# The down products of two ConvFFN channel mixers, by seven products of quarter blocks instead of a plain sum

## The chip, the cores and the metric

The kernel runs on one core of a Trainium2 chip. The metric is the device time of one execution in microseconds (us); lower is better. The engines are named as in the profile: PE (matrix products), DVE (vector), ACT (activations), POOL (GpSimd), and SP, whose queue issues the DMA transfers here.

## The reference

Two layers run over 1024 prompt frames and 64 sample frames (T = 1088 columns in the kernel, features on the partitions). Each layer is a token mixer (S5 in layer 0, forgetting attention in layer 1) followed by the channel mixer, with an RMSNorm in front of each and one at the end. The channel mixer is what the change touches:

```python
D_MODEL, D_FF = 1024, 2816
def conv_ffn(x, hist, w_up, w_gate, conv_w, conv_b, w_down):
    l = x.shape[1]
    a = x @ w_up
    a_pad = jnp.concatenate([hist.astype(a.dtype), a], axis=1)
    conv = a_pad[:, 0:l] * conv_w[0]
    for j in range(1, CONV_WIDTH):
        conv = conv + a_pad[:, j:j + l] * conv_w[j]
    h = jax.nn.gelu(conv + conv_b) * (x @ w_gate)
    return h @ w_down, a_pad[:, -(CONV_WIDTH - 1):]
```

All is float32. The kernel gets near float32 from the PE by splitting each operand into a high and a low part (`hi`, `lo`) and adding three matmuls: high by high, high by low, low by high.

## The kernel before

The 1088 columns are four chunks of 272 (`NCH`); columns 0 and 2 are half a = 0 and columns 1 and 3 half a = 1 (`HALVES`). The 2816 inner features are 22 tiles of 128 rows; two of them are a pair `fp`, so there are 11 pairs.

**Up and gate.** For each pair and for each of the two weights, `left_factors` loads 1024 x 256 weights into `raw` and makes the left factors of seven products of quarter blocks (the sums s1, a21, a11, a12 on POOL, each high part on ACT, each low part on POOL; the buffers `whi` and `wlo` hold three tiles each). `seven` runs the seven products for both halves a, so 14 products of 12 matmuls (4 slices of the inner dimension by 3), which share the PSUM banks A, B, G and H of each half. ACT copies bank A after products 0, 2 and 4 into a `tm` tile (5 buffers), and `put` adds a bank and a copy on DVE. Then `convolve` (DVE L424) and the gate product (L454) follow; the gated row h is split into a high part (ACT) and a low part (DVE L456), and both go to DRAM (`hD`), 0.557 MB each.

**Down.** `load` brings the rows back into the tiles `E` and `R` (28 in all), which hold the normalised input of up and gate until the last gate product has read them. The 22 tiles are taken in chunks of 3 (the last of 4, `FCH`); for each chunk, each of 8 output tiles d and each column chunk n, `down_tile` sums 9 (or 12) matmuls in one bank and DVE adds it to the residual x (L482). In the last chunk the columns go outermost, and as soon as one column chunk is complete, `norm.add` sums its squares and `after(n)` yields the steps that work on it: in layer 0 `to_operands`, which makes the normalised operands of the next product (`qkv`); in layer 1 `final`, which scales, transposes and writes the output.

The order of instructions on each engine is set by a scheduler, not by the lines of the source: it moves a later product ahead of an earlier one where it sees fit. SP issues the transfers in one queue, in order.

Of the kernel before, what the change touches and what calls it, by code (L numbers as in the profile page):

```python
# [16 lines left out]
P = 128  # L17
# [11 lines left out]
FCH = ((0, 3), (3, 3), (6, 3), (9, 3), (12, 3), (15, 3), (18, 4))  # L29
# [114 lines left out]
class Norm:  # L144
# [55 lines left out]
    def to_operands(self, i, g):  # L200

        k = self.k
        nc = k.nc
        o, n = NCH[i]
        r = self.inverse(i)
        yield
        yield
        pb = self.spread(i, r)
        for d in range(KT):
            t = k.tmp.tile([P, CW], F32, name="tm")[:, :n]  # L210
            nc.vector.scalar_tensor_tensor(t, k.x[d][:, o:o + n], k.gains[:, g, d:d + 1], pb, op0=OP.mult, op1=OP.mult)
            h = k.xh[d][:, o:o + n]
            nc.scalar.activation(h, t, AF.Copy)
            (nc.gpsimd if d % 4 else nc.vector).tensor_tensor(k.xl[d][:, o:o + n], t, h.bitcast(F32), op=OP.subtract)
# [76 lines left out]
def left_factors(k, w, c0):  # L291
# [3 lines left out]
    raw = k.wraw.tile([P, KT, 2 * P], F32, name="raw")  # L295
    nc.sync.dma_start(raw, w[:, c0:c0 + 2 * P].rearrange("(k p) c -> p k c", p=P))
    a11, a12, a21, a22 = (raw[:, 4 * i:4 * i + 4, P * f:P * f + P] for f in range(2) for i in range(2))

    def split(t, pools, shape, name):
        h, l = (q.tile(shape, F32R, name=name[i]) for i, q in enumerate(pools))  # L300
        nc.scalar.activation(h, t, AF.Copy)  # L301
        add(l, t, h.bitcast(F32), op=OP.subtract)  # L302
        return [[(h[:, 4 * i + kt], l[:, 4 * i + kt]) for kt in range(4)] for i in range(shape[1] // 4)]

    pair = (k.whi, k.wlo), [P, KT, P], ("hi", "lo")
    p1, p2 = split(raw[:, :, 0:P], *pair)
    s1 = k.idle[:, 0:4 * P].rearrange("p (a b) -> p a b", b=P)
# [4 lines left out]
    p6, p3 = split(raw[:, :, 0:P], *pair)  # L312
    p7, p4 = split(raw[:, :, P:2 * P], *pair)
    p5, = split(s1, (k.ws, k.ws), [P, 4, P], ("s1h", "s1l"))
# [3 lines left out]
def seven(k, left, halves, put, steps=None):  # L318
# [11 lines left out]
    def product(j, a, bank):  # L330
        more = j in (2, 4, 6)
        for kt in range(4):
            h, l = left[j][kt]
            rh, rl = (k.form(j, p, a)[:, kt] for p in range(2))
            for i, (x, y) in enumerate(((h, rh), (h, rl), (l, rh))):
                nc.tensor.matmul(bank[:, :CW], x, y, start=not more and kt == 0 and i == 0, stop=kt == 3 and i == 2, skip_group_check=True)  # L336
# [33 lines left out]
def ffn(k, layer, norm, after, prepare=lambda: None):  # L370
# [4 lines left out]
    hD = [k.dram.tile([2, P, T], F32, name=f"hD{layer}_{f}") for f in range(FT)]  # L375
    NX = 4
    cw = k.cw[layer]
    with ExitStack() as ctx:
# [6 lines left out]
        E, R = [(k.E[2 * i], k.E[2 * i + 1]) for i in range(6)], [(k.R[2 * i], k.R[2 * i + 1]) for i in range(8)]  # L385
        slots = E + R + E[:2] + R[:2] + E[2:]

        def load(fs):
            for f in fs:
                for t, src in zip(slots[f], (hD[f][0], hD[f][1])):  # L390
                    nc.sync.dma_start(t.bitcast(F32), src)

        def down_unit(ci, u, to=None):
            f0, nf = FCH[ci]
            src = w_down[f0 * P:(f0 + nf) * P, :].rearrange("(f p) c -> p f c", p=P)
            return unit(k, src[:, :, 2 * u * P:2 * (u + 1) * P], nf, 2 * P, to=to)

        def channels(fp, steps):
# [33 lines left out]
            if steps is not None:  # L432
                seven(k, left_factors(k, w_up, c0), ((0,),), put_up, steps)
                seven(k, left_factors(k, w_gate, c0), ((0,), (1,)), put_gate)
# [1141 lines left out]
```

## Time before, and how its profile reads

| | |
|---|---|
| median of 3 runs | 2755.19 us (2753.61 to 2761.34) |
| profiled execution: time, span | 2759.6 us, 2757.8 us |
| PE busy | 2632.0 us, 95% of the span |
| DVE, POOL, ACT busy | 57%, 53%, 39% |
| up and gate of layers 0 and 1 | about 470 to 977 and 1980 to 2460 us |
| down of layers 0 and 1 | about 977 to 1250 and 2460 to 2745 us |

The last two lines are rounded from the first and last instructions of `seven` and of `down_tile`. A share of busy time is a mean over stages with different limits, so it has to be asked for by stage. A wait counts only where PE stands still for it.

### The profile page before, as it was taken

The page shows a single profiled execution, that of the slowest core. Times are in us where ns is not written, and L with a number is a line of the kernel's source. Part 1 is how long each engine was busy: PE and PEld are TensorE (multiplying, and loading weights), DVE is VectorE, ACT ScalarE, POOL GpSimd, SP SyncE. Part 2 cuts the span into 40 slices and gives each one's busy share as a digit, 9 for nine tenths or more (in the row PEclk, how much of TensorE's full clock was granted, in tenths as well). Part 3 has the DMA queues.
Part 4 walks back from the last instruction along what each step waited for, and adds up shares of the span by engine and source line. Part 5 has one row for each costly group of instructions (what it writes and reads, how often), then busy time and mean ns, then how long its engine had stood idle before and what let it go on. Part 6 is the DMA issues. An engine that isn't in the chain of part 4 may idle for free. (4 is left out here: it accounts for less than half of the span.)

```text
span 2757.8 us, 52693 instructions
## 1 busy us (share of the span) xinstructions
PE 2632.0 (95%) x21030; PEld 2479.0 (90%) x21030; DVE 1563.6 (57%) x2986; ACT 1071.5 (39%) x2134; POOL 1466.7 (53%) x1110
## 2 busy tenths in 40 slices
PE   7987999899999999999999999999889999999998
PEld 4776999899999999999999866669889999999998
DVE  5898235676566633344322288873776666563335
ACT  5553333454444410023222277773344444430013
POOL 4675446786676621235222277764887776742223
PEclk8887999999999999999999999999899999999999
DMA  5123523132332393115685677753223232366211
GB/s 151 40 51 62 155 89 113 47 111 96 110 111 84 130 353 128 49 39 171 178 226 163 189 176 193 191 151 106 76 79 125 81 112 99 107 261 237 87 49 66
DMA packets 262985, 347.41 MB, mean 126 GB/s; under 512 B 32908, under 2 KB 217220, under 8 KB 262740
## 3 DMA queue, kind: packets, MB, share of 16 engines
q1 hardware_dynamic: 262740, 344.04, 40.4%
q8 instruction: 166, 2.72, 0.4%
q14 instruction: 79, 0.65, 0.1%
HBM read 232.37 MB, written 102.56 MB: 121 GB/s over the span
## 5 line engine op out<-in xcount | busy, mean ns | idle before, releaser
L123 POOL TENSOR_TENSOR lo<-raw,hi 128x1024 fp32r<-128x1024 f32 (+2 forms) x127 | 278.3, 2195 | 634.4 <-ACT hi L122 587.6
L302 POOL TENSOR_TENSOR lo<-raw,hi 128x1024 fp32r<-128x1024 f32 x138 | 377.2, 2736 | 208.3 <-ACT hi L301 208.2
L133 PE MATMUL mm<-xh,hi 128*128 128x272 f32 x1664 | 482.8, 291 | 2.7 <-ACT hi L122 1.1
L135 PE MATMUL mm<-xh,lo 128*128 128x272 f32 x1664 | 480.1, 290 | 2.7 <-POOL lo L123 2.7
L134 PE MATMUL mm<-xl,hi 128*128 128x272 f32 x1536 | 444.2, 290 | 0.0
L482 DVE TENSOR_TENSOR x<-x,mm 128x272 f32<-128x272 f32 x448 | 193.1, 436 | 303.2 <-PE mm L135 273.4
L336 PE MATMUL mm<-e,hi 128*128 128x272 f32 x1760 | 344.2, 291 | 7.8 <-ACT tm L340 7.2
L133 PEld LDWEIGHTS mm<-xh,hi 128*128 128x128 f32 x1664 | 315.8, 190 | 3.9 <-DVE tm L1384 1.5
L135 PEld LDWEIGHTS mm<-xh,lo 128*128 128x128 f32 x1664 | 314.6, 190 | 3.4 <-POOL lo L123 3.4
L122 ACT ACTIVATE hi<-raw 128x1024 fp32r<-128x1024 f32 (+2 forms) x127 | 122.9, 972 | 499.5 <-PE mm L134 388.1
L336 PE MATMUL mm<-xh,hi 128*128 128x272 f32 x1408 | 280.3, 293 | 21.9 <-DVE x L409 14.0
L134 PEld LDWEIGHTS mm<-xl,hi 128*128 128x128 f32 x1536 | 291.9, 190 | 0.1
L336 PEld LDWEIGHTS mm<-e,hi 128*128 128x128 f32 x1760 | 278.9, 190 | 8.8 <-ACT tm L340 7.5
L336 PE MATMUL mm<-e,lo 128*128 128x272 f32 x880 | 256.0, 291 | 2.8 <-POOL lo L302 2.8
L336 PEld LDWEIGHTS mm<-xh,hi 128*128 128x128 f32 x1408 | 226.4, 192 | 24.0 <-DVE x L409 14.9
L133 PE MATMUL mm<-e,hi 128*128 128x272 f32 x704 | 206.6, 294 | 11.3 <-issue 10.5
L336 PE MATMUL mm<-xh,lo 128*128 128x272 f32 x704 | 206.3, 294 | 0.0
L336 PE MATMUL mm<-xl,hi 128*128 128x272 f32 x1056 | 205.5, 289 | 0.0
L134 PE MATMUL mm<-e,hi 128*128 128x272 f32 x704 | 204.4, 291 | 0.0
L135 PE MATMUL mm<-e,lo 128*128 128x272 f32 x704 | 202.3, 291 | 0.0
L424 DVE SCALAR_TENSOR_TENSOR x<-x,cw,x 128x1090 f32<-128x1090 f32 x88 | 193.8, 2218 | 12.8 <-ACT x L422 12.0
L301 ACT ACTIVATE hi<-raw 128x1024 fp32r<-128x1024 f32 x138 | 145.0, 1053 | 92.8 <-PE mm L336 79.4
(408 smaller groups left out, 6591.3 us busy)
## 6 DMA issues: line engine op xcount, KB each, us to landing
e<-hD SPq DMA_DIRECT2D x48, 544.0 KB
raw<-in_ffn_w_up SPq DMA_DIRECT2D x24, 1024.0 KB
hD<-b SPq DMA_DIRECT2D x44, 544.0 KB
raw<-in_ffn_w_gate SPq DMA_DIRECT2D x22, 1024.0 KB
hD<-x SPq DMA_DIRECT2D x44, 512.0 KB
raw<-in_ffn_w_down SPq DMA_DIRECT2D x48, 384.0 KB
raw<-in_ssm_w_glu SPq DMA_DIRECT2D x112, 128.0 KB
xh<-hD SPq DMA_DIRECT2D x24, 544.0 KB
```

What stands on the lines that cost most here:

```text
L122: nc.scalar.activation(hi, raw, AF.Copy)
L123: nc.gpsimd.tensor_tensor(lo, raw, hi.bitcast(F32), op=OP.subtract)
L133: mm(ps, h, rh, start=first, stop=False)
L134: mm(ps, h, rl, start=False, stop=False)
L135: mm(ps, l, rh, start=False, stop=last)
L301: nc.scalar.activation(h, t, AF.Copy)
L302: add(l, t, h.bitcast(F32), op=OP.subtract)
L336: nc.tensor.matmul(bank[:, :CW], x, y, start=not more and kt == 0 and i == 0, stop=kt == 3 and i == 2, skip_group_check=True)
L424: v.scalar_tensor_tensor(c, ab[i][:, r:r + T + 2], cw[:, r, f:f + 1], c, op0=OP.mult, op1=OP.add)
L482: v.tensor_tensor(x, x, ps[:, :m], op=OP.add)
```

## The change

In `ffn`, the down products go by the same seven products as up and gate. The inner dimension and the 1024 output features are each cut in halves; a quarter block of the weights is one 128-row tile of a pair by 512 outputs.

- After the gate, `store_forms` makes the seven forms of the gated pair (the right factors), each split into a high part (ACT L438) and a low part (DVE L439; POOL for one of the seven) of 544 columns, and stores them in `fD`: seven transfers of 0.557 MB for each pair, where four tiles of that size went before.
- Down takes the pairs in chunks of two (`PCH`), the last chunk is one pair. A chunk's 14 form tiles are loaded into R[2:] or into E and two spare tiles, in turn. `down_unit` loads the weights of a chunk for 2 of the 4 pairs of output tiles and calls `left_factors`; each `down` is one `seven` with 14 products of 6 matmuls, and its results are two DVE additions each: x plus the bank (L537), then x plus the ACT copy (L538).
- In the last chunk a product has 3 matmuls, the halves a go outermost, the second addition is on POOL, all additions of `norm.add` are on DVE, and `after` works on a half (two column chunks) at a time.
- `qkv` takes its columns in the order of the halves.

```diff
-FCH = ((0, 3), (3, 3), (6, 3), (9, 3), (12, 3), (15, 3), (18, 4))
+PCH = ((0, 1), (2, 3), (4, 5), (6, 7), (8, 9), (10,))
 def left_factors(k, raw, X, C):
     add = nc.gpsimd.tensor_tensor
+    a11, a12, a21, a22 = (raw[:, X * i:X * i + X, C * f:C * f + C] for f in range(2) for i in range(2))
...
 def ffn(k, layer, norm, after, prepare=lambda: None):
-    hD = [k.dram.tile([2, P, T], F32, name=f"hD{layer}_{f}") for f in range(FT)]
+    fD = [k.dram.tile([7, P, T], F32, name=f"fD{layer}_{i}") for i in range(FP)]
...
+        def load(ci):
+            if ci % 2:
+                more = [k.big.tile([P, T], F32R, name="b") for i in range(2)] if len(PCH[ci]) > 1 else []
+                tiles = k.E + more
+            else:
+                tiles = k.R[2:]
+            for j in range(7):
+                for n, fp in enumerate(PCH[ci]):
+                    t = slots[fp, j] = tiles[7 * n + j]
+                    nc.sync.dma_start(t.bitcast(F32), fD[fp][j])
...
+        def store_forms(fp, gs, stage):
+            b11, b12, b21, b22 = (g[:, H * t:H * t + H] for g in gs for t in range(2))
+            def split(j, t):
+                q = stage()[:, :T]
+                nc.scalar.activation(q[:, :H].bitcast(F32R), t, AF.Copy)
+                (nc.gpsimd if j == 3 else v).tensor_tensor(q[:, H:], t, q[:, :H], op=OP.subtract)
+                nc.sync.dma_start(fD[fp][j], q)
+            split(0, b11)
+            split(1, b21)
+            split(5, b22)
+            v.tensor_tensor(b22, b22, b12, op=OP.subtract)
+            split(3, b22)
+            v.tensor_tensor(b12, b12, b11, op=OP.subtract)
+            v.tensor_tensor(b11, b22, b11, op=OP.add)
+            split(2, b11)
+            split(4, b12)
+            v.tensor_tensor(b21, b21, b11, op=OP.subtract)
+            split(6, b21)
...
-                    h = c[:, o + 2 * s:o + 2 * s + w]
-                    v.tensor_tensor(h, h, gs[i][:, o:o + w], op=OP.mult)
-                    nc.scalar.activation(hh[:, o:o + w], h, AF.Copy)
-                    v.tensor_tensor(h, h, hh[:, o:o + w].bitcast(F32), op=OP.subtract)
-                    nc.sync.dma_start(D[1, :, o:o + w], h)
-                nc.sync.dma_start(D[0], hh.bitcast(F32))
+                    v.tensor_tensor(g[:, o:o + w], c[:, o + 2 * s:o + 2 * s + w], g[:, o:o + w], op=OP.mult)
+            store_forms(fp, gs, lambda: next(turn)())
...
+            def put(f, th, a, bank, copy):
+                o, m = NCH[HALVES[a][th]]
+                x = k.x[d + 4 * f][:, o:o + m]
+                v.tensor_tensor(x, x, bank[:, :m], op=OP.add)
+                eng.tensor_tensor(x, x, copy, op=OP.add)
+            seven(k, [[f(x, c) for x in range(X)] for f in left], right, halves, put)
+        for ci, fps in enumerate(PCH):
+            if ci + 1 < len(PCH):
+                load(ci + 1)
+            if len(fps) > 1:
+                for u in range(2):
+                    unit = down_unit(ci, u) if ci or u else unit0
+                    for dd in range(2):
+                        down(unit, 2 * u + dd, dd * P, fps, ((0, 1),), v)
+                continue
+            unit = down_unit(ci, 0)
+            for a, hs in enumerate(HALVES):
+                for d in range(4):
+                    down(unit, d, d * P, fps, ((a,),), nc.gpsimd)
+                    for dt in (d, d + 4):
+                        for n in hs:
+                            norm.add(n, dt, True)
```

How the instructions stand now, at three places.

First, SP's queue where down begins (layer 0). `e_...`, `xh_...` and `xl_...` are tiles of E and R, `hD_n` the row tile n, `fD_n` the forms of pair n, `x<-xD` the residual coming back. Before:

```order
L391 DMA e_3051<-hD_0_5298 128x1088
L391 DMA e_3050<-hD_0_5298 128x1088
L508 DMA x_10707<-xD 128x1088
L391 DMA xh_1441<-hD_7_5305 128x1088 x2
L118 DMA raw<-in_ffn_w_down 128x3x256
L391 DMA e_3052<-hD_1_5299 128x1088
L391 DMA e_3053<-hD_1_5299 128x1088
L508 DMA x_10708<-xD 128x1088
```

and now, the last seven rows up to the first tile of pair 1 that PE needs and the next ones:

```order
L418 DMA e_3057<-fD_3_5301 128x1088
L418 DMA e_3056<-fD_2_5300 128x1088
L429 DMA raw<-in_ffn_w_down 128x2x256
L418 DMA xl_1730<-fD_1_5299 128x1088
L418 DMA xl_1442<-fD_0_5298 128x1088
L418 DMA e_3059<-fD_3_5301 128x1088
L418 DMA e_3058<-fD_3_5301 128x1088
L418 DMA xl_2306<-fD_1_5299 128x1088
L418 DMA xl_2018<-fD_1_5299 128x1088
```

Before, the first chunk's rows hD_0 to hD_2 stood among the first. Now the E tiles of the second chunk (fD_2, fD_3) stand between those of the first chunk (fD_0, fD_1); the first tile of pair 1 comes behind 16 tiles and 4 weight blocks, the last 12 places later.

Second, DVE behind a gate in the steady stretch, where `b` are the two gate tiles and staging tiles, and L465 and L471 the puts of up and gate (`mm` is a bank). Before, between the last puts of a gate and the first of the next up:

```order
L454 TENSOR_TENSOR x_7579<-x_7579,b 128x1024
L454 TENSOR_TENSOR x_7579<-x_7579,b 128x64
L415 TENSOR_TENSOR b<-mm,tm 128x272 x2
L456 TENSOR_TENSOR x_7579<-x_7579,b 128x1024
L456 TENSOR_TENSOR x_7579<-x_7579,b 128x64
L456 TENSOR_TENSOR x_7585<-x_7585,b 128x64
L454 TENSOR_TENSOR x_7585<-x_7585,b 128x1024
L456 TENSOR_TENSOR x_7585<-x_7585,b 128x1024
L409 TENSOR_TENSOR x_7896<-mm,tm 128x272 x2
```

and now:

```order
L439 TENSOR_TENSOR x_8364<-b,x_8364 128x544
L439 TENSOR_TENSOR b<-b 128x544
L465 TENSOR_TENSOR x_8457<-mm,tm 128x272
L445 TENSOR_TENSOR b<-b 128x544
L447 TENSOR_TENSOR b<-b 128x544
L465 TENSOR_TENSOR x_8457<-mm,tm 128x272
L448 TENSOR_TENSOR b<-b 128x544
L451 TENSOR_TENSOR b<-b 128x544
L439 TENSOR_TENSOR x_8379<-b,x_8379 128x544
L439 TENSOR_TENSOR b<-b 128x544
L465 TENSOR_TENSOR x_8459<-mm,tm 128x272
L439 TENSOR_TENSOR x_8388<-b,x_8388 128x544
```

The four subtractions of L456 have become ten operations on 544 columns, which reach into the puts of the next up.

Third, POOL at the end of down in layer 0. `xl<-tm,xh` (L214, now L217) are the low parts of the next operands, `lo` (L123, now L125) those of the next weights. Before:

```order
L123 TENSOR_TENSOR lo<-raw,hi 128x1024
L165 TENSOR_TENSOR s<-s,tm 128x272 x6
L214 TENSOR_TENSOR xl_1730<-tm,xh_1441 128x272
L214 TENSOR_TENSOR xl_2018<-tm,xh_1441 128x272
L214 TENSOR_TENSOR xl_2306<-tm,xh_1441 128x272
```

and now, from the last additions of half 1 but one:

```order
L538 TENSOR_TENSOR x_10598<-x_10598,tm 128x272
L125 TENSOR_TENSOR lo<-raw,hi 128x1024
L538 TENSOR_TENSOR x_3034<-x_3034,tm 128x272
L125 TENSOR_TENSOR lo<-raw,hi 128x1024
L538 TENSOR_TENSOR x_3034<-x_3034,tm 128x272
L538 TENSOR_TENSOR x_10598<-x_10598,tm 128x272
L538 TENSOR_TENSOR x_10903<-x_10903,tm 128x272
L538 TENSOR_TENSOR x_3035<-x_3035,tm 128x272 x2
L538 TENSOR_TENSOR x_10903<-x_10903,tm 128x272
L217 TENSOR_TENSOR xl_1730<-tm,xh_1441 128x272
```

The twelve low parts of half 0 follow that, then the additions of half 1's last outputs, and behind them the twelve low parts of half 1: POOL's 32 additions of the last chunk stand in one queue with the 24 low parts.

## Rows read from the trace of the kernel before

**Rows 1.** The page, busy time of each engine: us (share) x instructions.

```profile
PE 2632.0 (95%) x21030; PEld 2479.0 (90%) x21030; DVE 1563.6 (57%) x2986; ACT 1071.5 (39%) x2134; POOL 1466.7 (53%) x1110
```

**Rows 2.** Two stretches: length, then busy us (instructions) by engine, PE clock, DMA.

```profile
620.00:900.00 280.00, 280.00 (x2227) 280.00 (x2226) 176.37 (x198) 123.39 (x213) 194.04 (x105) 1.00 0.30 102
1100.00:1200.00 100.00, 100.00 (x798) 100.00 (x797) 38.66 (x89) 9.74 (x11) 21.37 (x11) 1.00 0.17 54
```

**Rows 3.** Windows of 10 us where PE stands still; last are DMA share, GB/s.

```profile
1000.00:1010.00 10.00, 9.21 (x74) 8.99 (x73) 1.76 (x4) 0.84 (x1) 1.83 (x1) 1.00 0.86 289
1010.00:1020.00 10.00, 5.05 (x36) 4.86 (x36) 1.48 (x4) 1.69 (x2) 3.12 (x2) 0.87 1.04 404
1020.00:1030.00 10.00, 10.00 (x66) 10.00 (x66) 4.36 (x11) 0.85 (x1) 0.52 (x2) 0.79 0.82 311
1250.00:1260.00 10.00, 9.21 (x72) 8.83 (x70) 7.86 (x19) 6.55 (x17) 9.69 (x8) 1.00 0.96 301
1260.00:1270.00 10.00, 6.97 (x32) 6.98 (x33) 2.67 (x9) 0.73 (x4) 1.93 (x3) 0.66 0.55 183
2490.00:2500.00 10.00, 7.83 (x63) 7.61 (x61) 0.00 (x0) 0.00 (x0) 0.42 (x1) 1.00 0.98 348
2500.00:2510.00 10.00, 6.65 (x33) 6.68 (x34) 4.10 (x11) 1.68 (x2) 3.58 (x2) 0.66 1.03 408
```

**Rows 4.** Timeline at the last gate of layer 0: SP's issues, PE's first down product.

```profile
957.06 0.80 SPq L391 DMA_DIRECT2D e<-hD  x2
...
961.17 1.89 SPq L391 DMA_DIRECT2D xh<-hD  x2
...
976.66 0.37 PE L133 MATMUL mm<-e,hi 128*128 128x272 f32 x1
```

**Rows 5.** DMA issues: count, KB each.

```profile
e<-hD SPq DMA_DIRECT2D x48, 544.0 KB
```

**Rows 6.** Single lines: ns minimum/median/maximum, first and last start, form.

```profile
L302 POOL TENSOR_TENSOR lo<-raw,hi x138: 2357/2499/3468, 477.3 to 2441.3; 128x1024 fp32r<-128x1024 f32 x138
L301 ACT ACTIVATE hi<-raw x138: 1039/1059/1065, 473.8 to 2440.2; 128x1024 fp32r<-128x1024 f32 x138
L308 POOL TENSOR_TENSOR s<-raw x46: 1269/1314/2372, 470.9 to 2415.1; 128x512 f32<-128x512 f32 x46
L482 DVE TENSOR_TENSOR x<-x,mm x448: 421/437/441, 982.8 to 2744.4; 128x272 f32<-128x272 f32 x150
L165 POOL TENSOR_TENSOR s<-s,tm x62: 757/772/1357, 305.4 to 2741.6; 128x272 f32<-128x272 f32 x62
L165 DVE TENSOR_TENSOR s<-s,tm x50: 420/443/2405, 316.0 to 2745.4; 128x272 f32<-128x272 f32 x50
L214 POOL TENSOR_TENSOR xl<-tm,xh x24: 758/774/981, 1224.8 to 1281.9; 128x272 fp32r<-128x272 f32 x24
L424 DVE SCALAR_TENSOR_TENSOR x<-x,cw,x x88: 1340/2258/3517, 549.2 to 2446.6; 128x1090 f32<-128x1090 f32 x88
```

**Rows 7.** Groups by form, 600 to 950 us (first) and 985 to 1300 us.

```profile
L454 DVE TENSOR_TENSOR x<-x,b 128x64 f32<-128x64 f32 x16 | 24.7, 1541 | 0.3
...
L123 POOL TENSOR_TENSOR lo<-raw,hi 128x1024 fp32r<-128x1024 f32 x7 | 17.2, 2461 | 18.2 <-ACT hi L122 18.2
```

**Rows 8.** Timeline: DVE and POOL at 2739 us; DVE alone at 731 us.

```profile
2739.38 1.24 DVE L165 TENSOR_TENSOR s<-s,tm 128x272 f32<-128x272 f32 x1 [1.16 <-ACT tm L164]
...
2739.04 1.28 POOL L1494 TENSOR_TENSOR raw<-raw,b 128x512 f32<-128x512 f32 x1 [1.39 <-ACT raw L1492]
...
731.72 1.23 DVE L456 TENSOR_TENSOR x<-x,b 128x1024 f32<-128x1024 f32 x1 [1.13 <-ACT b L455]
```

**Rows 9.** Timeline of DVE at the end of the program.

```profile
2744.41 0.42 DVE L482 TENSOR_TENSOR x<-x,mm 128x272 f32<-128x272 f32 x1
...
2749.59 0.75 DVE L1496 SCALAR_TENSOR_TENSOR raw<-mm,nr,b 128x512 f32<-128x512 f32 x1 [0.21 <-DVE nr L187]
...
2754.05 0.74 DVE L1496 SCALAR_TENSOR_TENSOR raw<-mm,nr,b 16x512 f32<-16x512 f32 x1 [2.29 <-DMA out_y_prompt<-raw]
```

More of the change, by code (lines that the diff above doesn't have):

```diff
@@ L311, in left_factors, with left_columns, seven @@
     add(a12, a12, a11, op=OP.subtract)
-    p6, p3 = split(raw[:, :, 0:P], *pair)
-    p7, p4 = split(raw[:, :, P:2 * P], *pair)
-    p5, = split(s1, (k.ws, k.ws), [P, 4, P], ("s1h", "s1l"))
+    p6, p3 = pair(0)
+    p7, p4 = pair(1)
+    p5, = split(s1, [k.ws.tile([P, 4, P], F32R, name=m) for m in ("s1h", "s1l")], 1)
     return p1, p2, p6, p7, p5, p3, p4
-def seven(k, left, halves, put, steps=None):
+def left_columns(k, w, c0):
+    raw = k.wraw.tile([P, KT, 2 * P], F32, name="raw")
+    k.nc.sync.dma_start(raw, w[:, c0:c0 + 2 * P].rearrange("(k p) c -> p k c", p=P))
+    return [[f(x, 0) for x in range(4)] for f in left_factors(k, raw, 4, P)]
+def seven(k, left, right, halves, put, steps=None):
     nc = k.nc
@@ L331, in product @@
         more = j in (2, 4, 6)
-        for kt in range(4):
-            h, l = left[j][kt]
-            rh, rl = (k.form(j, p, a)[:, kt] for p in range(2))
+        last = len(left[j]) - 1
+        for n, (h, l) in enumerate(left[j]):
+            rh, rl = (right(j, p, a, n) for p in range(2))
             for i, (x, y) in enumerate(((h, rh), (h, rl), (l, rh))):
-                nc.tensor.matmul(bank[:, :CW], x, y, start=not more and kt == 0 and i == 0, stop=kt == 3 and i == 2, skip_group_check=True)
+                nc.tensor.matmul(bank[:, :CW], x, y, start=not more and n == 0 and i == 0, stop=n == last and i == 2, skip_group_check=True)
     def copy(bank):
@@ L383, in ffn @@
             nc.sync.dma_start(k.xD[d], k.x[d])
[L385 to L396, printed above, removed]
+        slots = {}
@@ L484, in down, with right @@
[L484 to L500 removed]
+        def down(unit, d, c, fps, halves, eng):
+            X, left = unit
+            def right(j, part, a, x):
+                o = H * part + CW * a
+                return slots[fps[x], j][:, o:o + CW]
+            def put(f, th, a, bank, copy):
[4 more added lines that the diff above has]
+            seven(k, [[f(x, c) for x in range(X)] for f in left], right, halves, put)
@@ L503, in down @@
                     pass
[L504 removed]
+                steps = after(a)
             k.entry = steps
[L507 to L515 removed]
 SG = 64
@@ L1118, in qkv, with project @@
         last = ctx.enter_context(tc.tile_pool(name="qxs", bufs=1))
[L1120 to L1121 removed]
+        def project(u, evac):
+            for n in HALVES[0] + HALVES[1]:
                 o, m = NCH[n]
@@ L1543, in body @@
             prepare, after = final(k, norm)
-            ffn(k, 1, norm, after, prepare)
+            ffn(k, 1, norm, lambda a: itertools.chain(*(after(n) for n in HALVES[a])), prepare)
             for _ in k.entry:
```

127 lines of the change are left out of this document (55 added, 72 removed).

## The prediction

> **What bounds the kernel now.** I read the page first: PE is busy 95% of the span, every other engine under 60% [rows 1]. Then the windows by stage, because a share of the whole hides the stages. In the steady stretch of up and gate PE is busy 280 of 280 us and runs 2227 matmuls, and in the middle of down 798 in 100 us [rows 2], at the granted clock of 1.00, the upper of the two levels (2.4 GHz). That is 125.5 ns for each matmul of 272 columns, in both. So PE bounds both stages, and the reader should see at the same time how different the others are: in up and gate POOL is busy 69% and DVE 63%, in down 21% and 39%. The change thus takes PE work from the stage in which the other engines have room, and gives it the work that up and gate has. Then I looked for the places where PE stands still already: the first 20 to 30 us of down in both layers, and the passage from down to the next product [rows 3].
>
> **What it takes away.** Before, down is 22 tiles x 8 outputs x 4 chunks x 3 = 2112 matmuls in a layer; now 11 pairs x 4 outputs x 2 halves x 7 x 3 = 1848. That is 528 fewer in the two layers, at 125.5 ns [rows 2]: **-66.3 us**. The Trainium skill (TensorE: Matmul & The Clock Gate, Back-to-back issue gap) gives columns / 2.4 + 2.5 ns for a matmul at the upper clock, 115.8 ns here by my estimate, which would make it -61.2 us. The rows of this kernel have the same shape, so I keep theirs.
>
> **The start of down.** SP's order puts 17 tiles and 4 weight blocks up to the first tile of pair 1. A tile is 544 KB, 0.557 MB [rows 5], 1.37 us at the 406 GB/s that the transfers reach there (404 and 408 in the windows from 1010 and 2500 [rows 3]); a block of 0.262 MB is 0.65 us. Before, the last gate began 168 x 125.5 ns = 21.1 us before the first down product at 976.66, at 955.6; the first two loads went out 1.5 us after that, the next 5.6 us after [rows 4], and I take the transfers as gapless from there. So the first tile of pair 1 lands about 5.6 + 15 x 1.37 + 4 x 0.65 = 28.8 us after the gate began. The gate lasts 21.1 us, and the scheduler has put 24 matmuls (3.0 us) on pair 0 alone behind it: PE stands 4.7 us. The next tile that it needs is 4 places later, 5.5 us, with 12 matmuls (1.5 us) in front: 4.0 us more; then one more place (0.3 us), and three places (4.1 us) with 21 matmuls between: 1.5 us. Sum 10.5, and 2.5 us for the slow clock after it: before, 1000 to 1030 us lost 63 matmuls against 79.7 in 10 us, 8 us, of which PE idled only 5.7, and the granted clock fell to 0.87 and 0.79. Both layers lost 8 us before [rows 3]; now 13. **+10 us**; from 0 (if the order's fillers hide it) to +25 (transfers at 300 GB/s, as in the window from 1250).
>
> **Steady down.** Who holds whom has to be settled first. A DVE addition of two SBUF tiles takes 0.42 us alone, but up to 2.4 [rows 6]. The one at 2739.38 began while POOL ran an operation from 2739.04 to 2740.32, and ended at 2740.62, 0.30 us behind it [rows 8]. So the two exclude each other, and the DVE operation holds the other off for some 0.30 us; an addition with a bank as operand is never longer than 0.441 [rows 6]. By the same difference, 1024 columns (1.23 alone [rows 8]) hold 1.11, 544 columns 0.59 (between the two), the 1090 of L424 1.22. POOL's low part of 1024 holds 2.36, its other operations of 512 hold 1.27 [rows 6].
>
> A weight unit of down is 168 matmuls, 21.1 us. POOL has 3 x 2.36 + 5 x 1.27 = 13.4, DVE's 16 second additions 16 x 0.30 = 4.8: 18.2 of 21.1 us, it fits. But while POOL works, one put passes for each POOL operation: 8 puts in 13.4 + 8 x 0.30 = 15.8 us, the other 8 at 0.437 + 0.30 in 5.9: 21.7 us, 0.6 too many. The weights have their own chain: the first `whi` tile is free 60 matmuls (7.5 us) before the unit ends; ACT 1.06, low part 2.36, two sums 2.54, the low part of s1 1.27, the next low part 2.36 make 9.6, with five DVE holds 11.1 [rows 6]; PE asks for it after 7.5 + 31 matmuls = 11.4 us. It just fits, so 0 to 1 us. I take 1.0 us for each of the 20 units: **+20 us**, bounds 0 and +40.
>
> **Up and gate.** A pair is 336 matmuls, 42.2 us. POOL: 26.8 plus one subtraction (about 1.35, from 512 columns up) = 28.2. DVE's operations on two SBUF tiles: four of L424 4.9, two products 2.4, ten of 544 columns 5.9 = 13.2. Together 41.4 of 42.2 us, where before it was 36.5 (26.8, the same 4.9, and two products and two subtractions 4.8). A 64-column product took 1.54 us on average there already [rows 7]. PE has room in the banks (the bank that is put last is written again three products of 3 us later), so I expect mostly none, but the x tiles that convolve writes are now staging tiles too, and a late DVE holds ACT's L422 and the copies behind it. I take 0.5 us for each of 22 pairs: **+11 us**, bounds 0 and +33. The extra transfers (1.7 MB for a pair, +40 GB/s on 102 [rows 2]) lie far under 414 GB/s and cost nothing.
>
> **The last chunk.** It is 168 matmuls, 21.1 us, where it was 384, so what follows each output has less cover. Layer 0: until qkv has its operands POOL has 32 additions of 0.77, 24 low parts of 0.774 [rows 6] and 3 of 2.46 [rows 7], 50.6 us, and DVE holds it 36 x 0.30 = 10.8: 61.4 us, with 5.2 us in which the reciprocal root leaves it idle (the end of the program shows that gap, 2744.41 to 2749.59 [rows 9]): 66.6. PE has 168 + 192 matmuls in that stretch, 45.2 us: it waits 21, where it lost 55 matmuls, 7 us, before (1250 to 1270 [rows 3]). +14, bounds +5 and +25. Layer 1: DVE has 32 first additions of 0.437, 28 of norm.add at 0.42 or more and 9 output operations of 0.75 [rows 6, 9], 32.6 us, and waits for POOL's 0.77 (mean 0.27 x 28 = 7.5): 40.1 against 21.1, bounds 11.5 and 22, I take +17. Then two column chunks instead of one are left behind the last addition: six output tiles, of which two go in 4.46 us [rows 9]: +6, bounds 0 and +7. Together **+37 us**, bounds +16 and +54.
>
> **The sum.** -66.3 + 10 + 20 + 11 + 37 = +11.7 us on the profiled execution's 2759.6; its median of runs is 4.4 lower, and on that it is 2755.2 + 11.7 = 2767 us. What a measurement of this kernel can tell from no change is about 0.3%, 8.3 us.
>
> **Rivals.** *The engines have room after all (faster).* The holds fit on paper in both steady stretches (18.2 in 21.1, 41.4 in 42.2), PE lost nothing at 36.5, and the scheduler moves matmuls that need only the high part ahead. Then the two steady terms are 0: 2755.2 - 66.3 + 10 + 37 = 2736, with the last chunk at its lower bound 2715. It decides at the place where L538 stands behind POOL: if PE's count in 100 us of down stays at 797. *DVE and POOL become the bound of up and gate (slower).* If POOL is never idle, each of DVE's 18 operations on two SBUF tiles passes behind one of POOL's: 28.2 + 13.2 + 18 x 0.12 = 43.6 us for a pair, and if a fifth of its 7 us of puts does not hide under POOL, 45. That is +2.8 for 22 pairs, 62 in place of 11: 2818. For it speaks that 41.4 is 98% of 42.2, against it that PE lost nothing at 86%. The Trainium skill (SBUF — State Buffer, Who interferes with whom) states this rule: a DVE operation with two SBUF inputs and a GpSimd operation that reads SBUF exclude each other for the whole instruction, one with a single SBUF input does not wait. By that rule the change puts its additions on the wrong pair of engines; the trace agrees on the exclusion ([rows 8]), and no stretch of it is as full as 98%. *The first loads are slower (slower).* At 300 GB/s the waits at both starts grow by some 10 us each: 2787. That the matmuls don't go is excluded by the order.
>
> **Chances.** The forecast, 2748 to 2796, 0.42, of it 0.19 within 0.3% and 0.23 slower. The first rival 0.30, nearly all faster. The second 0.20, the third 0.08. So faster 0.30, within 0.3% 0.20, slower 0.50. The terms' bounds add to far more than can fall together; 2715 takes in the first rival at its lower bound, 2825 the second, and what lies outside is under 0.2. The forecast's own range is 2748 to 2796.
>
> **What would show it.** PE's matmuls fall by 528. Right for the steady terms: 100 us windows of down with 750 to 790 matmuls, DVE over 80% busy, L538 with a median well over 0.42. Wrong: 797 in down and in up and gate. Right for the last chunk: POOL over 85% busy for 50 us at the end of down in layer 0 with PE under 75%, and 20 us or more from the last addition to the end. At the start of down PE's longest waits should end on `xl` tiles from `fD_1`. I am wrong if PE keeps its pace behind the gate while DVE is above 90%: then a late DVE costs nothing and the gain of 66 us stands but for the ends.

## The result, and the profile after

The changed kernel takes **2977.63 us** (median of 4 runs, 2971.10 to 2979.82) where the kernel before took 2756.2 us on the same chip: ratio 1.0797, 95% interval 1.0774 to 1.0820. It is 8% slower; the forecast was 2767 us with a range of 2748 to 2796, and the slowest rival reached 2825. The profiled span grew from 2757.8 to 2976.2 us, by 218.4.

The page, busy time by engine, as [rows 1], and the granted clock in 40 slices:

```profile
PE 2664.0 (90%) x20502; PEld 2475.0 (83%) x20502; DVE 1993.9 (67%) x3404; ACT 1235.9 (42%) x2520; POOL 1768.9 (59%) x1286
...
PEclk8887999999999999977999999999899999999997
```

The 528 matmuls are gone (21030 to 20502), yet PE's busy time rose from 2632.0 to 2664.0 us. The mean granted clock of the span fell from 0.967 to 0.940, and a matmul that stands alone beside a stall counts as 0.29 us busy, one in a row as 0.1255. Two events that stand in every one of the kernels here cut the span into stages: the transposition of `tail` behind the last gate product (L515, before L462), and the first transposition in `qkv` (L1184, before L1135). In us, worked out from their starts:

| profiled execution | gate of layer 0 ends | down of layer 0 and passage | to the end of gate in layer 1 | down of layer 1 and output | span |
|---|---|---|---|---|---|
| before | 976.6 | 312.6 | 1172.1 | 296.5 | 2757.8 |
| after | 1024.4 | 373.3 | 1224.0 | 354.5 | 2976.2 |
| growth | 47.8 | 60.7 | 51.9 | 58.0 | 218.4 |

So about 92 us were lost in up and gate (45.5 and 46.9 between the first up matmul and the last gate product of a layer), and 119 in the two downs, which by their matmuls alone should have become 66 shorter. Windows of the changed kernel, to be held against [rows 2] (steady up and gate, steady down), and 10-us windows of the start of down and of the last chunk, against [rows 3]:

```profile
660.00:960.00 300.00, 280.41 (x2178) 275.30 (x2178) 223.53 (x238) 132.88 (x230) 212.04 (x111) 1.00 0.37 136
1064.00:1274.00 210.00, 185.81 (x1365) 182.29 (x1366) 166.73 (x263) 63.67 (x129) 118.51 (x67) 0.94 0.53 188
...
1020.00:1030.00 10.00, 7.16 (x55) 6.72 (x54) 8.84 (x9) 2.83 (x4) 5.74 (x3) 0.99 1.03 410
1030.00:1040.00 10.00, 6.30 (x26) 5.25 (x26) 7.15 (x7) 2.40 (x6) 3.45 (x2) 0.67 1.03 408
1040.00:1050.00 10.00, 9.85 (x64) 9.63 (x65) 4.59 (x12) 2.62 (x5) 0.72 (x1) 0.83 1.02 400
1050.00:1060.00 10.00, 9.17 (x73) 8.95 (x72) 9.97 (x14) 4.72 (x10) 8.58 (x6) 1.00 0.56 194
...
1114.00:1124.00 10.00, 7.12 (x42) 6.90 (x43) 6.71 (x10) 0.79 (x2) 4.56 (x3) 0.83 0.36 110
...
1314.00:1324.00 10.00, 3.78 (x12) 2.49 (x11) 2.79 (x5) 3.58 (x10) 5.60 (x8) 0.50 0.00 1
```

Up and gate does 2178 matmuls in 300 us, 46.3 us for a pair of 336, where 42.2 is PE's pace. Down does 1365 in 210 us, 25.8 us for a weight unit of 168, where 21.1 is the pace. At that pace 1365 matmuls are 171.3 us, so 38.7 are lost; PE idled only 24.2 of them (210 - 185.81). Of the other 14.5, 10.4 are the lower level of the clock: by the trace's start times and its granted clock 103 of the matmuls ran at it, behind stalls, 0.227 us apart on average. The rest is busy time as the profile counts it beside stalls; in up and gate, at a clock of 1.00, it is likewise 7.1 us above 2178 x 125.5 ns.

The matmuls behind each gate can also be counted off in groups of 168 by their start times. In layer 0 the first group takes 34.5 us, the next nine 232.9 (25.9 each), and from the last chunk's first matmul to `qkv` pass 105.9; in layer 1 35.2, 235.6, and 83.6 to the end of the program.

PE's longest waits in the whole program (us, times, longest); then PE's only waits in the steady down (1064 to 1274 us) and in up and gate (640 to 960); then the second addition L538, whose neighbour L537 reads a bank (ns minimum/median/maximum; by form in 1064 to 1274 us, the last numbers are busy us and mean ns):

```profile
PE mm L348 <- ACT tm L352: 98.8, 69, 7.2
PE mm L348 <- DVE x L537: 60.0, 44, 2.9
PE mm L348 <- DVE x L465: 19.7, 6, 4.2
...
PE mm L348 <- DVE x L537: 25.9, 16, 2.9
...
PE mm L348 <- ACT tm L352: 19.3, 15, 1.5
```

```profile
L538 DVE TENSOR_TENSOR x<-x,tm x320: 425/442/2644, 1042.3 to 2898.7; 128x272 f32<-128x272 f32 x160
...
L538 DVE TENSOR_TENSOR x<-x,tm 128x272 f32<-128x272 f32 x132 | 120.4, 943 | 15.7 <-ACT tm L352 13.8
L537 DVE TENSOR_TENSOR x<-x,mm 128x272 f32<-128x272 f32 x129 | 53.5, 430 | 27.6 <-PE mm L348 27.0
```

Both additions do the same work, but the one with two SBUF inputs takes 943 ns on average against 430. The timeline of a steady unit shows on what it waits. DVE first, then POOL, then ACT, then PE:

```profile
1162.41 3.91 DVE L538 TENSOR_TENSOR x<-x,tm 128x272 f32<-128x272 f32 x2
1166.24 0.42 DVE L537 TENSOR_TENSOR x<-x,mm 128x272 f32<-128x272 f32 x1
1166.59 3.74 DVE L538 TENSOR_TENSOR x<-x,tm 128x272 f32<-128x272 f32 x2
...
1162.16 2.40 POOL L304 TENSOR_TENSOR lo<-raw,hi 128x1024 fp32r<-128x1024 f32 x1 [1.33 <-PE mm L348]
1164.53 1.49 POOL L304 TENSOR_TENSOR s1l<-s,s1h 128x512 fp32r<-128x512 f32 x1
1165.97 2.59 POOL L304 TENSOR_TENSOR lo<-raw,hi 128x1024 fp32r<-128x1024 f32 x1
...
1182.43 2.62 POOL L304 TENSOR_TENSOR lo<-raw,hi 128x1024 fp32r<-128x1024 f32 x1 [10.98 <-ACT hi L303]
...
1166.43 0.40 ACT L352 ACTIVATE tm<-mm 128x272 f32<-128x272 f32 x1 [1.65 <-DVE x L538]
1170.44 0.40 ACT L352 ACTIVATE tm<-mm 128x272 f32<-128x272 f32 x1 [3.61 <-DVE x L538]
...
1170.73 0.52 PE L348 MATMUL mm<-xh,hi 128*128 128x272 f32 x2 [1.46 <-DVE x L537]
```

Two additions take 3.91 us while POOL runs one low part after the other, and two more 3.74. The next L537, which reads a bank that PE needs again, stands behind them in DVE's order and comes at 1170.25; PE has stood for it since 1169.27. ACT's copies wait too (3.61 us for a `tm` tile that such an addition still holds), but in the steady down all of PE's waits end on L537, none on a copy. After this burst POOL sits idle 10.98 us. That its work comes in bursts because PE, standing still, releases the weight tiles late is a reading, not shown by itself.

In up and gate PE's waits end on ACT's copies instead, some twice in each pair. One stop, ACT then PE:

```profile
846.26 0.66 ACT L438 ACTIVATE x<-b 128x544 fp32r<-128x544 f32 x1 [3.37 <-DVE b L509]
...
847.37 0.38 ACT L352 ACTIVATE tm<-mm 128x272 f32<-128x272 f32 x1
...
847.80 0.52 PE L348 MATMUL mm<-xh,hi 128*128 128x272 f32 x2 [1.44 <-ACT tm L352]
```

ACT stands 3.37 us with the high part of a form (L438) before DVE's late gate product (L509), and the copy comes behind it. The other stop of this pair looks the same, with ACT's L481 behind DVE's convolution (L480).

### The profile page after: what moved, and what is told of

The parts are those of the page before. It is cut to its first block, busy times and chain, and to the rows that moved or that the text cites. A ratio compares the mean times of both kernels' runs of the same rounds, so it can differ in the third digit from the quotient of the medians.

```text
span 2976.2 us, 53153 instructions
## 1 busy us (share of the span) xinstructions
PE 2664.0 (90%) x20502; PEld 2475.0 (83%) x20502; DVE 1993.9 (67%) x3404; ACT 1235.9 (42%) x2520; POOL 1768.9 (59%) x1286
## 5 line engine op out<-in xcount | busy, mean ns | idle before, releaser
L304 POOL TENSOR_TENSOR lo<-raw,hi 128x1024 fp32r<-128x1024 f32 x204 | 537.7, 2639 | 427.6 <-ACT hi L303 417.8
L348 PE MATMUL mm<-e,hi 128*128 128x272 f32 x2592 | 524.2, 299 | 74.0 <-ACT tm L352 45.0
L348 PEld LDWEIGHTS mm<-e,hi 128*128 128x128 f32 x2592 | 420.8, 196 | 85.0 <-ACT tm L352 47.4
L348 PE MATMUL mm<-e,lo 128*128 128x272 f32 x1296 | 380.2, 299 | 2.7 <-POOL lo L304 2.7
L352 ACT ACTIVATE tm<-mm 128x272 f32<-128x272 f32 x552 | 205.9, 387 | 414.5 <-PE mm L348 338.4
L125 POOL TENSOR_TENSOR lo<-raw,hi 128x1024 fp32r<-128x1024 f32 (+2 forms) x73 | 174.2, 2392 | 258.1 <-ACT hi L124 249.9
L538 DVE TENSOR_TENSOR x<-x,tm 128x272 f32<-128x272 f32 x320 | 284.8, 921 | 35.2 <-ACT tm L352 30.6
L348 PEld LDWEIGHTS mm<-xl,hi 128*128 128x128 f32 x1728 | 280.4, 195 | 19.5 <-DMA xl<-fD 8.7
L348 PEld LDWEIGHTS mm<-e,lo 128*128 128x128 f32 x1296 | 254.4, 199 | 3.7 <-POOL lo L304 3.6
L348 PE MATMUL mm<-xl,lo 128*128 128x272 f32 x864 | 252.1, 294 | 0.0
L136 PEld LDWEIGHTS mm<-xl,hi 128*128 128x128 f32 x1280 | 244.9, 192 | 0.8 <-POOL xl L217 0.6
L480 DVE SCALAR_TENSOR_TENSOR x<-x,cw,x 128x1090 f32<-128x1090 f32 x88 | 168.8, 1936 | 74.0 <-ACT x L478 73.3
```

Of the source, the lines that this page charges most:

```text
L125: nc.gpsimd.tensor_tensor(lo, raw, hi.bitcast(F32), op=OP.subtract)
L136: mm(ps, h, rl, start=False, stop=False)
L348: nc.tensor.matmul(bank[:, :CW], x, y, start=not more and n == 0 and i == 0, stop=n == last and i == 2, skip_group_check=True)
L352: nc.scalar.activation(t, bank[:, :CW], AF.Copy)
L480: v.scalar_tensor_tensor(c, ab[i][:, r:r + T + 2], cw[:, r, f:f + 1], c, op0=OP.mult, op1=OP.add)
L538: eng.tensor_tensor(x, x, copy, op=OP.add)
```

## The experiments

The theories. For down, **T1**: the additions of two SBUF tiles and POOL's operations exclude each other, so they come late. **T2**: the banks and copied tiles are held through two additions, whatever these read. For up and gate, **U1**: ACT's order, behind a store; **U2**: the exclusion there. For the last chunk, **L1**: copies queue in ACT's order behind squares; **L2**: the chain of one bank; **L3**: POOL's additions. Each ratio is to the kernel before on the same chip, and points are hundredths of that ratio; the stages are read as in the table above.

**The second addition reads a bank.** In `put`:

```diff
-                eng.tensor_tensor(x, x, copy, op=OP.add)
+                eng.tensor_tensor(x, x if len(fps) == 1 else bank[:, :m], copy, op=OP.add)
```

> In the five chunks of two pairs the second addition of each quarter (copy onto the residual) becomes bank plus copy, so that one of its two inputs lies in PSUM; it holds the bank and the copied tile exactly as long as before. This changes part of the computation: the residual loses what it held, and the bank's quarter is counted once. Now a weight unit of the steady down takes about 25.7 us (1374 matmuls in 210 us from 1064 on, at 168 to a unit), where 168 matmuls by 125.5 ns are 21.1. Theory T1 (DVE's additions with both inputs in SBUF and POOL's operations on the weights exclude each other, so the additions come late and PE stops for them): the unit falls to 21.5 to 22.5 us, in 20 units 65 to 85 us, so about 2900 (2885 to 2925). Rival T2 (it is the holding of banks and of the five copied tiles through two additions in a row, whatever their operands): no change, 2965 or more.

2875.82 us, ratio 1.0404 (1.0380 to 1.0429), 3.9 points below the changed kernel. The addition, and a stretch inside the steady down of the changed kernel and, last, of this one (whose last chunk begins at 1252):

```profile
L538 DVE TENSOR_TENSOR x<-mm,tm x320: 422/440/444, 1042.5 to 2798.4; 128x272 f32<-128x272 f32 x160
...
1084.00:1240.00 156.00, 138.50 (x1011) 135.91 (x1010) 122.39 (x196) 48.37 (x100) 87.51 (x49) 0.93 0.53 191
...
1084.00:1240.00 156.00, 156.00 (x1247) 155.98 (x1246) 95.91 (x236) 59.09 (x119) 102.14 (x60) 1.00 0.53 195
```

None of the 320 additions is longer than 444 ns, though POOL does the same work, PE is busy all of the time, and from the third unit on a unit takes 21.0 to 21.3 us: the whole loss of the steady down is gone. The two downs fell from 373.3 and 354.5 to 322.5 and 309.3; of these 96 us some 16 lie in the last chunk and behind it, where nothing was edited. T1 is shown for the steady down, T2 falls: banks and tiles are held through two additions as before. (The scheduler's order changed with it, in about a tenth of PE's instructions.) The Trainium skill (SBUF — State Buffer, Who interferes with whom) says that a DVE operation with at most one SBUF input, outside the modes that use both ports, does not contend with GpSimd; this run agrees, 444 ns against 2644.

**Additions straight from the bank.** In `seven`, for the steady chunks:

```diff
                 if j in (0, 2, 4):
-                    c[j] = copy(b["A"])
+                    for f, th in {0: ((0, 0),), 2: ((1, 0),), 4: ((1, 1), (0, 1))}[j]:
+                        put(f, th, a, b["A"], None)
```

> In the same five chunks the intermediate sums of bank A are not copied out by ACT at all: DVE adds bank A to the residual as soon as product 0, 2 or 4 is in it (four additions of a bank for each half of the columns instead of four of a copied tile), and the finished banks B, G, H, G as now. The whole computation stands. As many DVE additions as now (32 to a weight unit, 32 x 0.43 = 13.8 us of 21.1), none with two inputs in SBUF, no copied tiles; in exchange bank A waits for DVE instead of ACT before product 2 and product 4 may go on. T1: the unit falls to 21.5 to 22.5 us, 2885 to 2925. T2: it falls as well, for no copied tile is left to hold. Third, T3 (DVE has too many additions in its order whatever they read, and PE waits for DVE): the unit stays at 25 us or grows, 2965 or more.

2896.29 us, ratio 1.0487 (1.0453 to 1.0520), down 333.7 and 316.2; from the third unit on 21.0 to 21.3 us a unit. T1 again, T3 falls: as many additions, from banks, do not hold PE up. It is slower than the kernel of the run above at the start: the first two units of layer 0 take 67.4 us against 57.5, and there DVE waits 10.8 us for a tile of the residual (`x<-xD`), while bank A now waits for DVE.

**Low parts of the forms as copies by ACT.** In `store_forms`:

```diff
-                (nc.gpsimd if j == 3 else v).tensor_tensor(q[:, H:], t, q[:, :H], op=OP.subtract)
+                nc.scalar.activation(q[:, H:], t, AF.Copy)
```

> The low parts of the seven forms of the gated rows are written by ACT as a copy of the full value, not by DVE and POOL as value minus high part: part of the computation is changed. That takes six operations with two SBUF inputs from DVE and one from POOL in each pair of up and gate, and gives ACT seven of about 0.65 us. A pair now takes 45.9 us where its matmuls take 42.2. U2 (in up and gate the mutual exclusion of DVE and POOL, which sums to 41.4 us a pair, sets the pace): the pair falls to 42.5 to 43.5 us, in 22 pairs 50 to 75 us, so about 2915 (2900 to 2930). U1 (ACT stands in its order before the first operation of the convolution, which waits for the store of a form out of the tile it writes, and the copies of the banks queue behind it): no gain, 2965 to 3000, with ACT 4.5 us a pair fuller.

2925.06 us, ratio 1.0585 (1.0548 to 1.0623): 2.1 points, 58 us of 2756. The gate of layer 0 ends at 995.3, and 2287 matmuls in the window of 660 to 960 make 44.1 us a pair. So the low parts on DVE and POOL cost 2.2 of the 4.1 us a pair. That is what U2 said, but the edit takes DVE time away together with the exclusion, and no run here parts the two in up and gate as the bank did in down; 1.9 us a pair stay.

**Another rotation of the staging tiles.**

```diff
-            turn = itertools.cycle((lambda: xtile(k, 2), lambda: xtile(k, 3), lambda: k.big.tile([P, T], F32, name="b")))
+            turn = itertools.cycle((lambda: k.big.tile([P, T], F32, name="b"), lambda: xtile(k, 2), lambda: xtile(k, 3)))
```

> The seven forms of a pair rotate through three tiles as now, but begin with the large one, so that the last form no longer lies in the tile that the next pair's convolution writes first. The computation is whole. In the profile ACT's line 478 waited 40.4 us in 20 waits for the store out of that tile, about 1.9 us a pair. U1: those waits go and with them 1 to 2 us of PE's loss in each of 22 pairs: 2935 to 2955. U2: nothing changes, 2970 to 2985.

2961.13 us, ratio 1.0717 (1.0685 to 1.0749), 0.8 points. PE's waits for ACT's copies fell from 98.8 to 69.3 us, but those for DVE's L465 rose from 19.7 to 45.6: 2199 matmuls in the window instead of 2178. The store wait is a small part, and most of what it frees turns into a wait for DVE.

**The last chunk: squares one row later; additions from the banks; second additions on DVE.** All three stand on the direct kernel, where a row is a seven-product group of one pair of output tiles and one half. In ACT's order in that kernel's last chunk, one row lies between two L352 after three squares:

```profile
1273.04 1.07 ACT L166 ACTIVATE tm<-x 128x272 f32<-128x272 f32 x3 [1.46 <-POOL x L544]
1274.01 0.38 ACT L352 ACTIVATE tm<-mm 128x272 f32<-128x272 f32 x1
1275.53 0.40 ACT L352 ACTIVATE tm<-mm 128x272 f32<-128x272 f32 x1 [1.14 <-PE mm L348]
1277.06 0.40 ACT L352 ACTIVATE tm<-mm 128x272 f32<-128x272 f32 x1 [1.14 <-PE mm L348]
1277.36 0.42 ACT L166 ACTIVATE tm<-x 128x272 f32<-128x272 f32 x1
1279.24 1.07 ACT L166 ACTIVATE tm<-x 128x272 f32<-128x272 f32 x3 [1.46 <-POOL x L544]
1280.21 0.38 ACT L352 ACTIVATE tm<-mm 128x272 f32<-128x272 f32 x1
```

The squares (L166) wait 1.46 us for POOL's additions, and the next row's first copy starts only behind them; PE's next matmul came at 1274.44, having waited 3.62 us for it. The edits:

```diff
+                for d in range(5):
+                    if d < 4:
+                        down(unit, d, d * P, fps, ((a,),), nc.gpsimd)
+                    if d:
+                        for dt in (d - 1, d + 3):
...
-            seven(..., direct=len(fps) > 1)
+            seven(..., direct=True)
...
-                    down(unit, d, d * P, fps, ((a,),), nc.gpsimd)
+                    down(unit, d, d * P, fps, ((a,),), v)
```

> On top of the direct additions of the steady chunks: in the last chunk the squares for the norm of a row of tiles are given out one row later, behind the copies of the next row, where they now stand ahead of them in ACT's order. In the direct kernel a row of the last chunk takes 6.2 us (ACT's copies of bank A at 1274.01, 1280.21 and 1286.41) for 21 matmuls, 2.6 us by 125.5 ns. Theory L1 (the copies stand in ACT's order behind squares that wait for POOL's additions, and PE waits for the copies): a row falls to 3.5 to 4.5 us, in 16 rows 27 to 43 us, so 2855 to 2870 against 2890 to 2896 of the direct kernel. Rival L2 (the chain matmul, copy, matmul of one bank and the half level of TensorE's clock set the row, whatever ACT has in its order): 0 to 10 us, 2880 to 2896. Rival L3 (POOL's additions at about 0.77 us, 4 a row, and DVE set the end, the norm's sums only come later): no change or slower, 2890 to 2910.

> The direct additions in the last chunk as well: DVE adds bank A to the residual, POOL adds nothing there and ACT copies nothing, while the squares for the norm stand where they stood. L1: the squares still wait, now for DVE's additions, but no copy stands behind them; PE waits for DVE before products 2 and 4, and DVE has 8 additions and 4 sums of squares a row, 12 x 0.43 = 5.2 us: the row falls to 5.2 to 5.7 us, 8 to 16 us in 16 rows, 2875 to 2888. L2: the bank is read back as late as now or later (two additions for product 4 instead of one copy): 2885 to 2905. L3: without POOL's additions the chain is shorter, 2870 to 2880.

> On top of the direct additions of the steady chunks: the second additions of the last chunk, of the copied tiles, go from POOL to DVE, and nothing else changes. L1: the squares wait for DVE's addition instead of POOL's, which is ready 0.3 us sooner each, so a row falls from 6.2 to about 5.5 us, 2880 to 2890. L3: POOL's 0.77 us were the bound, 12 to 25 us less, 2868 to 2882. L2: no change, 2886 to 2900.

Against 1.0487 of the direct kernel: squares later 1.0431 (1.0396 to 1.0466), additions from the banks 1.0377 (1.0354 to 1.0401), second additions on DVE 1.0469 (1.0431 to 1.0506). From the last chunk's first matmul to `qkv`, and in layer 1 to the end, the profiled executions took:

| us | layer 0 | layer 1 |
|---|---|---|
| direct kernel | 98.1 | 79.5 |
| squares later | 91.1 | 70.3 |
| additions from the banks | 86.7 | 65.6 |
| second additions on DVE | 95.4 | 75.9 |

So POOL's pace is not the bound (L3's reason falls: the third cannot be told from no change). Squares later gave 0.6 points, some 15 us, less than L1 said, and the intervals still touch (the profiled span fell by 19). Without copies it gave 1.1, 30 us, more than any of the three theories said; L2, by which it should have been no faster, falls. So part of the loss is the copy in ACT's order, about 25 us of both layers by the table; the larger part is not there.

**Three together** (additions from the banks in all chunks, squares later, rotation).

> Three changes at once, the computation whole: direct additions in all chunks, the squares of the last chunk one row later, and the rotation of the staging tiles that begins with the large one. If they add up by L1: 2890 to 2896 less 16 (rotation, as measured on the changed kernel) less 20 to 35 (last chunk) is about 2850 (2838 to 2866). By L2 only the rotation counts: 2870 to 2882.

2844.70 us, ratio 1.0297 (1.0270 to 1.0324), inside the range. The additions from the banks (1.0377) and the rotation (0.8 points) add up to it by themselves: the later squares give nothing on top (85.0 and 66.1 us in the terms of the table, after 86.7 and 65.6), as L1 has it, for no copy stands behind them any more. Down is 317.3 and 297.0, 4.7 and 0.5 above the kernel before, though the matmuls alone are 33 us less in each; the rest of what is left lies ahead of the two downs (38.1 and 40.7).

**And the low parts as copies, on top.**

> On top of the three changes together (2844.7 us, ratio 1.0297): the low parts of the forms are written by ACT as a copy of the full value, as in the earlier run on the changed kernel; part of the computation is changed. With the rotation of the tiles in it as well, both suspects of up and gate are gone. U2 with U1 as a separate part (exclusion and store wait each cost their own time): the full 50 to 58 us of the earlier run on top of the rotation's 16, the gate of layer 0 ends at 985 to 990 against 976.6 before the change, and the whole is 2785 to 2797. If the two are one slack (whichever is taken away first gives most): 20 to 40 us, 2805 to 2825.

2794.38 us, ratio 1.0120 (1.0091 to 1.0149), 1.8 points or 49 us, after 2.1 in the earlier run, so the low parts and the store wait are in the main separate costs; the gate of layer 0 ends at 992.3, later than I said (985 to 990), and 2302 matmuls from 660 to 960 make 43.8 us a pair, 1.6 above PE's pace.

**Split after the load.** The forms go to DRAM whole, by three stores from the gated tiles and four operations of DVE, and are split where down loads them:

```diff
+            store(0, b11)
+            store(1, b21)
+            store(5, b22)
+            v.tensor_tensor(q[:, :H], b22, b12, op=OP.subtract)
+            store(3, q[:, :H])
...
+            full, hi = t[:, H:].bitcast(F32), t[:, :H]
+            nc.scalar.activation(hi, full, AF.Copy)
+            (nc.gpsimd if key[1] in POOLED else v).tensor_tensor(t[:, H:], full, hi.bitcast(F32), op=OP.subtract)
```

> On top of the three changes together, the computation whole: the forms of the gated rows go to DRAM as full values (half the bytes, straight from the gated tiles or after one operation of DVE), and are split into high and low part after they are loaded, by ACT and by DVE or POOL, one at a time between the additions of the chunk before. Up and gate lose 14 ACT, DVE and POOL operations a pair, 7 of them with two SBUF inputs; a weight unit of the steady down gets 7 splits, about 0.7 us each on ACT and on DVE or 1.5 on POOL. U2 for up and gate: the gate of layer 0 ends at 980 to 990, together 50 to 70 us less. T1 for down: the new locked operations (4 of DVE by 0.72 and 3 of POOL by 1.5 us in a unit, with 11.4 us of POOL's on the weights 19 of 21.1 us) leave little room: 0 to 2 us a unit, 0 to 40 us in 20 units. Sum 2775 to 2835; if the holds of down come late as they did in the changed kernel, 5 us a unit, 2875 to 2895.

2856.08 us, ratio 1.0340 (1.0301 to 1.0379), between the two sums. Its steady windows, and 10 us of down:

```profile
660.00:960.00 300.00, 300.00 (x2386) 300.00 (x2385) 206.68 (x215) 119.95 (x201) 212.78 (x115) 1.00 0.29 97
...
1064.00:1274.00 210.00, 186.45 (x1394) 183.51 (x1393) 131.34 (x313) 57.01 (x81) 131.96 (x78) 0.94 0.28 86
...
1050.00:1060.00 10.00, 6.71 (x48) 5.83 (x46) 10.00 (x15) 5.19 (x7) 10.00 (x7) 1.00 0.25 83
```

Up and gate is back at PE's own pace, 42.2 us a pair, and its gate ends at 982.3: the splitting of the forms, with its stores of twice the size, was the whole of that stage's steady loss. But down takes 25.3 us a unit again, 358.2 and 335.3: what was taken from one stage came back in the other. The mean hides where: behind the first chunk each chunk's second unit runs at 21.0 to 21.5 us, and its first takes 27 to 33. The 14 splits for a later chunk stand there in one burst, DVE and POOL are both busy 10.00 of 10 us, and in layer 0 PE makes one long stop in each such unit: 4.5 us for an addition, then 7.1, 5.9 and 4.8 us for ACT's high parts of the weights.

> As the kernel that splits after the load, the computation whole, but the splits are given out only in the first of a weight unit's two rows of tiles (4 late in the first unit of a chunk, 10 in the second), where POOL and ACT are not yet at work on the next unit's weights. In the run before, up and gate ran at PE's own pace (2386 matmuls in 300 us at granted clock 1.00), and down lost 41 and 38 us more than with forms split ahead: PE waited for ACT's high parts of the weights, which stood behind splits that waited for their load. If that order is what cost it (T4): down returns to within 5 to 15 us of 317 and 297, so 2795 to 2815. If it is the sum of locked work in down (T1 again): no change, 2845 to 2865.

2853.11 us, ratio 1.0331 (1.0309 to 1.0354). This run settles nothing: the scheduler gave all engines the same order as in the kernel above, whatever the place in the source. T4 was so not tested, and whether late loads in ACT's order or the locked work of the burst bring down its 25.3 us stays open.

**The last pair by the plain sum.**

> As that kernel, but the last pair of gated rows is multiplied as in the kernel before the change: no seven products and no forms for it, 6 matmuls to a sum and one addition of DVE to each 272 columns, column chunks in the order 0 to 3 with the norm behind each (192 matmuls for 168 a layer, 24 x 125.5 ns = 3 us more). If the last chunk's loss comes from the short products with their many additions and from the norm for half of the columns at a time, down falls to about 290 and 270, 25 us a layer: 2745 to 2765, the level of the kernel before. If it comes from something else in the passage to the next stage: 2795 to 2815 as the one above.

2820.35 us, ratio 1.0227 (1.0192 to 1.0262), between the two values. In layer 1 the stretch from `qkv` to the end fell by 25.0 us (1515.6 to 1490.6), in layer 0 the stretch up to it did not (1340.1 to 1344.7): the profiled execution is 17 us above the median and 10 us late already at the end of layer 0's gate, with 374 matmuls in its first 100 us against 564. Counted from the end of each gate, the chunks of two pairs take 10.3 and 9.9 us less, half of it where the last pair's forms were split; the last pair and what follows take 5.0 us more in layer 0 and 10.4 less in layer 1. So this run does not show that the short products, or the norm for half of the columns at a time, carry most of the last chunk's loss. It is the fastest whole computation among these kernels; none beats the kernel before.

## Why the prediction was wrong, point by point

- **What bounds it, what it takes away.** Right: 528 matmuls fewer, and where PE was not held up a unit of 168 took some 21.1 us in every kernel. The 66 us are there, under the losses.
- **The start of down.** Right: 55, 26, 64 and 73 matmuls from 1020 to 1060 against 79.7 each are 101 lost, 12.7 us, where I said 13. Of PE's 7.3 us of waits there 3.6 end on the load of an `xl` tile, the longest (2.6) among them, as I had named it; the rest is the lower clock (0.67 and 0.83) and waits for weights and additions, so the size is better than its working. The first 168 matmuls of the two layers lose 27.5 us, where the first 384 lost 17.1 before: 10.4 more, for a forecast of 10.
- **Steady down, the step that failed.** I said 1.0 us a unit, from "one put passes for each POOL operation ... 21.7 us, 0.6 too many". It was 4.9 us a unit, 89 us in the 18 units behind the first ones, in place of 1.0 and 20. The mechanism was the right one (the second addition reading a bank takes all of it away). The sum was wrong in kind: it added the holds as if DVE and POOL always had work, which gives the least time, not the likely one. What it left out is DVE's order: the first additions, which PE waits for, stand behind the held ones, 16 stops and 25.9 us in 210, while POOL at other times sits idle, 10.98 us in the unit shown. And I priced the lower clock only at the start of down; here it is 10.4 of 38.7 us lost. The windows have 650 matmuls in 100 us (1365 in 210), below the 750 to 790 of my sign. My other sign, a median of L538 well over 0.42, was the wrong statistic: the median is 442 ns, the mean 943.
- **Up and gate, the same step.** 0.5 us a pair forecast, 46.3 - 42.2 = 4.1 measured, about 92 us with the ends against 11. "41.4 of 42.2 us" was read as room. The way I named was right (a late DVE holds ACT, and the copies queue behind it), and my second rival had 45 us a pair, 62 us; but it left out the store wait, and it was given 0.20. How much of it is the exclusion and how much DVE's added work alone stays open. Taking seven of the forms' operations away brings 44.1, taking all of the splitting away 42.2.
- **The last chunk, mis-sized by half.** From its first matmul on, layer 0 has 105.9 us for 21.1 of matmuls, where the last 384 had 87.3 for 48.2 before; layer 1 83.6 for 21.1, before 71.5 for 48.2. That is 84.9 us more lost in both, against 37. I had summed engines (66.6 us of POOL, 45.2 of PE); the rows show a chain through ACT's order of 6.2 us a row, for 21 matmuls of 2.6 us, at a clock of 0.50. My sign, POOL busy over 85% for 50 us, did not come: it is busy 29.88 of the 50 us from 1314. The 20 us from the last addition to the end did (2954.5 to 2976.2). The same 6.2 us stand in the changed kernel (first copies at 1313.15 and 1319.35). Of the 84.9 us 12 went with the direct additions of the steady chunks. Three together took 36 us from the two downs (649.9 in the direct kernel, 614.3 then), 27 of them here; the other 46 were not taken apart further.
- **Rivals and chances.** The case that steady down and up and gate both lose far more than their sums said had no chance of its own; it is what happened.

## What to carry to other kernels

When two engines exclude each other, the sum of their holds does not tell whether a stage has room. In up and gate 36.5 of 42.2 us (86%) cost nothing before the change and 41.4 cost 4.1 us a pair; in down 18.2 of 21.1 us, 86% again, cost 4.9 us a unit. Look in the order for what stands behind a held operation and who waits for it: here it was PE. Let an addition read one operand from PSUM where it can: that gave back 3.9 points here, and 3.1 with the computation whole. Before moving an operation out of a full stage, price it in the stage that receives it, and check in the order that the scheduler moved it at all.

## What was not expected of the hardware

In the steady down short stalls of PE cost about 0.4 of their length again in clock. PE's timeline in the changed kernel, two stalls in the steady down:

```profile
1116.45 1.02 PE L348 MATMUL mm<-e,hi 128*128 128x272 f32 x6 [2.58 <-DVE x L537]
...
1145.17 0.52 PE L348 MATMUL mm<-xh,hi 128*128 128x272 f32 x2 [2.59 <-DVE x L537]
```

The window from 1114 has 42 matmuls in 7.12 us of PE's time at a mean granted clock of 0.83, so part of it at the lower of the two levels, 1.2 GHz, and part at 2.4. Over the steady down, beside 24.2 us of idle time, 103 matmuls at the lower level took 10.4 us more than at the upper. In up and gate stalls of at most 1.5 us (19.3 us in 15 waits for copies, 640 to 960) left the clock at 1.00. But in the steady down stalls of 1.46 and 0.76 us close together, at 1169 and 1172, were followed by the lower level too.
